# Y's and the turn's products alternated on four quarters of the array, in the chunked recurrence of a two-layer decoder

## The chip, the cores and the metric

The kernel runs on one core of a Trainium2 chip. The metric is the device time of one execution in microseconds. A core has TensorE (PE; its weight loads are shown apart as PEld), VectorE (DVE), ScalarE (ACT), GpSimd (POOL) and SyncE (SP), which issues the DMAs here. TensorE multiplies a stationary operand (`lhsT`) with a moving one (`rhs`) and writes into PSUM; its array can be used in parts: rows follow the partitions of the operands, columns those of the output.

## The reference

A decoder trunk of two layers on 2048 tokens of 1024 channels in fp32: sliding-window attention, then RWKV-7 time mixing, each with a gated branch and a per-layer embedding. The change is in the second layer's recurrence, one 64x64 state for each of 16 heads:

```python
def step(S, inp):
    r_t, d_t, k_t, v_t, kk_t, a_t = inp
    sa = jnp.einsum('bhvk,bhk->bhv', S, -kk_t)
    S = S * d_t[:, :, None, :] + sa[..., None] * (kk_t * a_t)[:, :, None, :] + v_t[..., None] * k_t[:, :, None, :]
    y = jnp.einsum('bhvk,bhk->bhv', S, r_t)
    return S, y
...
mean = jnp.mean(y, axis=-1, keepdims=True)
var = jnp.mean(jnp.square(y - mean), axis=-1, keepdims=True)
y = ((y - mean) * lax.rsqrt(var + GN_EPS)).reshape(B, T, C) * gn_g.astype(jnp.float32) + gn_b.astype(jnp.float32)
bonus = jnp.sum(r4 * k4 * r_k.astype(jnp.float32), axis=-1, keepdims=True) * v4
y = (y + bonus.reshape(B, T, C)).astype(h.dtype)
return (y * jax.nn.silu(z)) @ w_out
```

## The kernel before

Four phases follow each other; the last, `rwkv` (line 1165), holds all that the diff touches but one line. It works in chunks of 64 tokens (`LC`), 32 of them (`NCH`). Channels lie on partitions, 128 to a tile, so a tile column p (8 of them, `NP`) holds two heads, one on each half of the partitions (`half`); h and eo number the halves.

Within a chunk the recurrence is solved in closed form, in small fp32 products. Each fp32 product is two matmul instructions on the chip, called passes below. `chain(c)` (line 1323) runs them: r1p from the state and the chunk's values (line 1329); the first part of y (1335); `turn` (1365), which transposes the normed y of the chunk before, `yc`, to channels on partitions; up, through the inverted triangle `tt` (1341); two copies of u into `uv`, one on VectorE and one on ScalarE (1342, 1343); sp, the state's update (1348), which VectorE and GpSimd carry on; and y's second part (1356). y's and the turn's and up's products are 64x64, with the rows and the columns of the same half; r1p, sp and y's second part use all rows and one half of the columns.

Three generators feed the chain. `front(c)` (1221) makes the chunk's products `aps` (16 passes for each of two halves of p) and transposes its keys; the chain needs it a chunk later. `tri(g)` (1253) inverts the triangles of four chunks: 30 steps of two VectorE operations (1269, 1271), then for each chunk a first and a second set of 32x32 products `wq` (1290, 1300) with copies `wt` and `tt` behind them, one half on ScalarE and one on VectorE. `output(c, y)` (1372) norms y, waits for its turn, multiplies by `gn_g` and adds and multiplies by `bvt` and `szt`, which `load_bz` (1360) loads, and stores `gated`.

Between these products stands the dense work of the layer, one step of three 128x128x512 matmuls at a time (`mm3`, lines 589 to 591), from `Dense.run` (143): the z projection, the output projection, the gate. `self.ticks(n)` lets every running generator make n steps, so `STEPS` (1321) says how many dense steps stand behind r1p, behind y and turn, behind up and behind the end of the chain: 18 for a chunk. `add_gate1` (403) has at line 418 a number of such steps between the gate's elementwise work and four transposes on TensorE.

The program is built with a plan by simulated time (line 1451): within an engine's queue instructions may be put ahead of others that the plan has waiting. Each queue then runs in that order. PSUM tiles of tag "f" come from 3 buffers, "ch" (r1p, up, sp) from 1, y from 1.

## Time and profile before

| what | value |
|---|---|
| median of 3 runs | 3070.1 us (3067.87 to 3070.78) |
| the profiled execution | 3072.72 us, span 3070.6 us |
| granted TensorE clock over the span | 0.969 |
| TensorE busy | 2865.7 us, 93% |
| VectorE busy | 1950.4 us, 64% |
| ScalarE, GpSimd busy | 43%, 33% |
| 16 DMA engines, hardware queue | 69.8% |

The share of an engine is over the whole span, with its four phases; what a change in one phase is worth is read from that phase. A row of the timeline gives the start in us from the span's start, the length in us, the engine, the line, the operation, what it writes and reads, shapes, and how many instructions were merged; its length runs to the end of the last one, and since matmuls are pipelined the next one starts before that. In brackets stands how long the engine was idle before and what it waited for. PEclk is the granted TensorE clock, 1.00 being 2.4 GHz.

### The profile page before, as it was taken

Reading aid. Unit: us, or ns where it says so; the run is one execution under the profiler, and the core shown is the slowest. Engines: PE = TensorE matmul, PEld = TensorE weight load, DVE = VectorE, ACT = ScalarE, POOL = GpSimd, SP = SyncE. Lnnn points to the kernel's source line nnn. Section 1 sums busy time; section 2 is a strip of 40 time slices with the busy share of each in tenths; the row PEclk is TensorE's granted clock in tenths of the full one; section 3 lists DMA queues with packets and bytes.
Section 4 is the critical chain, followed back from the end, with each engine's and each line's share of the span. In section 5 each row is a group of like instructions: output and inputs, shape, how many; then the busy total and the mean of one; then the engine's idle time right before and its main releaser. Section 6 shows DMA issues by size and latency. Waiting matters only on the chain. (4 is left out here: it accounts for less than half of the span.)

```text
span 3070.6 us, 56425 instructions
## 1 busy us (share of the span) xinstructions
PE 2865.7 (93%) x21416; PEld 2265.5 (74%) x21416; DVE 1950.4 (64%) x3529; ACT 1314.0 (43%) x2840; POOL 1005.2 (33%) x886
## 2 busy tenths in 40 slices
PE   7999998999999999898998799888989989999987
PEld 5888886777777777686776588666777767777766
DVE  6532434775777655738678965588685795784444
ACT  5311114784465543526677733322334433332422
POOL 2242510001211232404556600224445435435421
PEclk9999999999999999999999899999999999999999
DMA  7664857999886687636556778896779878679574
GB/s 224 187 144 107 167 142 224 308 284 335 253 258 207 214 270 244 192 114 199 176 190 197 213 209 207 244 285 177 190 198 253 217 228 242 170 209 249 164 250 158
DMA packets 622687, 652.41 MB, mean 212 GB/s; under 512 B 259152, under 2 KB 433360, under 8 KB 622416
## 3 DMA queue, kind: packets, MB, share of 16 engines
q1 hardware_dynamic: 614736, 638.31, 69.8%
q0 software_dynamic: 7680, 10.50, 3.1%
q8 instruction: 169, 2.77, 0.4%
q14 instruction: 102, 0.84, 0.1%
HBM read 421.39 MB, written 216.79 MB: 208 GB/s over the span
## 5 line engine op out<-in xcount | busy, mean ns | idle before, releaser
L589 PE MATMUL ps<-dhi,dwh 128*128 128x512 f32 x1472 | 610.1, 416 | 23.4 <-ACT dwh L538 9.9
L591 PE MATMUL ps<-dhi,dwl 128*128 128x512 f32 x1472 | 590.6, 402 | 11.5 <-DVE dwl L540 11.0
L590 PE MATMUL ps<-dlo,dwh 128*128 128x512 f32 x1472 | 592.6, 404 | 4.3 <-DVE dlo L540 2.4
L589 PE MATMUL ps<-xH,wh 128*128 128x512 f32 x1408 | 554.2, 400 | 17.7 <-DVE kb L1071 11.2
L590 PE MATMUL ps<-xL,wh 128*128 128x512 f32 x1408 | 560.2, 398 | 5.0 <-POOL xL L540 4.0
L591 PE MATMUL ps<-xH,wl 128*128 128x512 f32 x1408 | 561.2, 399 | 1.3 <-DVE wl L540 1.3
L589 PEld LDWEIGHTS ps<-dhi,dwh 128*128 128x128 f32 x1472 | 281.1, 191 | 95.5 <-ACT dwh L538 11.4
L591 PEld LDWEIGHTS ps<-dhi,dwl 128*128 128x128 f32 x1472 | 281.5, 191 | 78.5 <-DVE dwl L540 13.8
L590 PEld LDWEIGHTS ps<-dlo,dwh 128*128 128x128 f32 x1472 | 281.8, 192 | 61.8 <-DVE dlo L540 4.5
L589 PEld LDWEIGHTS ps<-xH,wh 128*128 128x128 f32 x1408 | 267.9, 191 | 80.4 <-DVE kb L1071 14.9
L590 PEld LDWEIGHTS ps<-xL,wh 128*128 128x128 f32 x1408 | 269.2, 191 | 67.4 <-POOL xL L540 7.3
L591 PEld LDWEIGHTS ps<-xH,wl 128*128 128x128 f32 x1408 | 269.0, 191 | 59.2 <-DVE wl L540 2.6
L699 POOL DMA_DIRECT2D t<-t x160 | 126.1, 1274 | 200.2 <-issue 75.6
L873 ACT ACTIVATE S<-S,nm 128x256 f32<-128x256 f32 (+1 forms) x256 | 125.5, 492 | 66.1 <-DVE nm L870 59.3
L540 POOL TENSOR_TENSOR xL<-xs,xH 128x512 fp32r<-128x512 f32 x72 | 109.8, 1535 | 76.0 <-ACT xH L538 73.0
L538 ACT ACTIVATE wh<-wr 128x1024 fp32r<-128x1024 f32 x44 | 46.6, 1059 | 190.9 <-DMA wr<-in_attn_w_in 144.9
L864 DVE CUSTOM_DVE_ANT_0 S<-sc,mask,sink 128x256 f32<-128x256 f32 (+1 forms) x256 | 108.7, 469 | 23.4 <-PE sc L860 23.2
L1269 DVE TENSOR_TENSOR tmp<-P 128x30 f32<-128x30 f32 (+14 forms) x240 | 111.7, 466 | 13.8 <-POOL P L1260 7.5
L1052 POOL TENSOR_TENSOR kb<-kb,mhalf 128x16 f32<-128x16 f32 x32 | 100.6, 3146 | 36.9 <-DVE kb L1051 36.6
L1271 DVE TENSOR_TENSOR P<-P,tmp 128x30 f32<-128x30 f32 (+14 forms) x240 | 108.2, 451 | 6.7
L975 DVE SCALAR_TENSOR_TENSOR xs<-hp,mu,xs 128x512 f32<-128x512 f32 x96 | 93.1, 986 | 28.8 <-ACT xs L974 28.5
L540 POOL TENSOR_TENSOR dlo<-z,dhi 128x512 fp32r<-128x512 f32 x16 | 22.3, 1408 | 258.8 <-ACT dhi L538 252.2
(258 smaller groups left out, 5211.6 us busy)
## 6 DMA issues: line engine op xcount, KB each, us to landing
hp<-hn SPq DMA_DIRECT2D x72, 256.5 KB, 4.3
sz<-th SPq DMA_DIRECT2D x64, 256.0 KB, 4.4
ple<-pt SPq DMA_DIRECT2D x64, 256.0 KB, 7.1
aux<-ple SPq DMA_DIRECT2D x64, 256.0 KB, 5.3
yd<-kx SPq DMA_DIRECT2D x32, 512.0 KB, 4.2
dwh<-wp_ao SPq DMA_DIRECT2D x24, 512.0 KB, 6.1
dwl<-wp_ao SPq DMA_DIRECT2D x24, 512.0 KB, 6.8
dwh<-wp_ag SPq DMA_DIRECT2D x24, 512.0 KB, 4.5
```

The source lines that it names most:

```text
L538: nc.scalar.activation(hi, src, AF.Copy)
L540: e.tensor_tensor(out=lo, in0=src, in1=f32(hi), op=ALU.subtract)
L589: mm(ps, lhsT=wh, rhs=ah, start=first, stop=False)
L590: mm(ps, lhsT=wh, rhs=al, start=False, stop=False)
L591: mm(ps, lhsT=wl, rhs=ah, start=False, stop=last)
L699: nc.gpsimd.dma_start(out=t1[32 * d:32 * d + 32, :], in_=t2[32 * a:32 * a + 32, :], accum_op=ALU.add)
L864: nc.vector.tensor_tensor_reduce(out=S[:, i, c0:], in0=sc[:, eo, c0:], in1=mask[:, c0:], scale=1.0, scalar=sink[:, 4 * g + 2 * j + eo:4 * ...
L873: nc.scalar.activation(S[:, i, c0:], S[:, i, c0:], AF.Exp, bias=nm[:, i:i + 1], accum_out=den[:, i:i + 1])
L975: nc.vector.scalar_tensor_tensor(out=src, in0=t[:, :G], scalar=mus[:, c, k:k + 1], in1=src, op0=ALU.mult, op1=ALU.add)
L1052: nc.gpsimd.tensor_tensor(out=bs[:, :, 0], in0=bs[:, :, 0], in1=self.mhalf.broadcast_to([128, m]), op=ALU.pow)
L1269: nc.vector.tensor_tensor(out=t, in0=P[:, 0:r, r:r + 1].broadcast_to([128, r, n]), in1=P[:, r:r + 1, r + 1:].broadcast_to([128, r, n]), op ...
L1271: nc.vector.tensor_tensor(out=P[:, 0:r, r + 1:], in0=P[:, 0:r, r + 1:], in1=t, op=ALU.add)
```

## The change

The y products and the turn's products are issued in turns, two of y (on the quarters of the diagonal) and two of the turn, and the turn writes its result to the other half of the partitions, so that it uses the two other quarters. What follows it lies with its halves swapped: `gn_g` has a swapped copy `gnx`, and `bvt`, `szt` and the store of `gated` are two DMAs each (`heads`); the last chunk keeps the old way. Up follows directly, without ticks between. The first half of `aps` of chunk c+2 is issued at the end of chain(c), behind y's second part, and the second half behind r1p of chain(c+1); y's second part and `aps` take half 1 first. The `wq` products of two chunks of a group are issued together, and their copies are all on ScalarE. `load_front` stands ahead of the chain, and the gate's transposes come two steps later.

```diff
@@ -415,7 +415,7 @@
             if ct == 0:
                 sums[n] = self.cp.tile([128, NB, KT], F32, name="ss", bufs=2)
             ss = sums[n]
-            for _ in range(4):
+            for _ in range(6):
                 yield
             for b in range(NB):
                 nc.tensor.transpose(ps[:, b * 128:b * 128 + 128], th[:, b * 128:b * 128 + 128], tr.ident)
@@ -1196,13 +1196,16 @@
             p_f, p_c, p_y = (self.pool(es, "pw_" + nm, b, PSUM) for nm, b in (("f", 3), ("c", 1), ("y", 1)))
             dense.transposed = lambda name: p_f.tile([128, G], F32, name=name, tag="f")
             gng = self.vec["gn_g"]
+            gnx = cp.tile([128, NP], F32, name="gnx")
             dl = self.decay
             if "decay" in self.override:
                 nc.sync.dma_start(out=dl, in_=self.override["decay"])
             S = cp.tile([128, NP, 64], F32, name="S0")
             nc.vector.memset(S, 0.0)
             half = (slice(0, 64), slice(64, 128))
-            AM, X1, XA, BN, TT, UV, AG, BZ, YC, YT = {}, {}, {}, {}, {}, {}, {}, {}, {}, {}
+            for h in range(2):
+                nc.sync.dma_start(out=gnx[half[1 - h]], in_=chan(ins["rwkv_gn_g"][0], NP)[half[h]])
+            AM, X1, XA, BN, TT, UV, AG, BZ, YC, YT, FR = {}, {}, {}, {}, {}, {}, {}, {}, {}, {}, {}
 
             def load_front(c):
                 x1 = X1[c] = x1p.tile([128, NP, 128], F32, name="x1")
@@ -1226,7 +1229,7 @@
                 for i in range(NP // 4):
                     pse = [p_f.tile([128, 4, 128], F32, name="aps", tag="f") for eo in range(2)]
                     for j in range(4):
-                        for eo in range(2):
+                        for eo in (1, 0):
                             nc.tensor.matmul(pse[eo][:, j], lhsT=x1[half[eo], 4 * i + j], rhs=xa[half[eo], 4 * i + j],
                                              start=True, stop=True)
                     for eo in range(2):
@@ -1281,28 +1284,27 @@
                 for e in range(2):
                     nc.gpsimd.memset(tt[64 * e + 32:64 * e + 64, :, :, 0:32], 0.0)
                 yield
-                for j in range(TG):
-                    wt = sm.tile([128, NP, 32], F32, name="wt")
+                for j in range(0, TG, 2):
+
+
+                    wt = sm.tile([128, 2, NP, 32], F32, name="wt")
                     wq = p_f.tile([128, 2, NP, 32], F32, name="wq", tag="f")
-                    for p in range(NP):
-                        for e in range(2):
-                            r0 = 64 * e
-                            nc.tensor.matmul(wq[r0 + 32:r0 + 64, 0, p], lhsT=ag[r0:r0 + 32, p, j, 32:64], rhs=at[r0:r0 + 32, p, j],
-                                             start=True, stop=True)
+                    ops = [(i, p, 64 * e) for i in range(2) for p in range(NP) for e in range(2)]
+                    for i, p, r0 in ops:
+                        nc.tensor.matmul(wq[r0 + 32:r0 + 64, i, p], lhsT=ag[r0:r0 + 32, p, j + i, 32:64], rhs=at[r0:r0 + 32, p, j + i],
+                                         start=True, stop=True)
                     for e in range(2):
-                        cpy = nc.vector.tensor_copy if e else nc.scalar.copy
-                        cpy(wt[64 * e + 32:64 * e + 64], wq[64 * e + 32:64 * e + 64, 0])
-                    yield
-                    yield
-                    for p in range(NP):
-                        for e in range(2):
-                            r0 = 64 * e
-                            nc.tensor.matmul(wq[r0:r0 + 32, 1, p], lhsT=wt[r0 + 32:r0 + 64, p], rhs=tt[r0 + 32:r0 + 64, p, j, 32:64],
-                                             start=True, stop=True)
+                        nc.scalar.copy(wt[64 * e + 32:64 * e + 64], wq[64 * e + 32:64 * e + 64])
+                    for _ in range(4):
+                        yield
+                    for i, p, r0 in ops:
+                        nc.tensor.matmul(wq[r0:r0 + 32, i, p], lhsT=wt[r0 + 32:r0 + 64, i, p], rhs=tt[r0 + 32:r0 + 64, p, j + i, 32:64],
+                                         start=True, stop=True)
                     for e in range(2):
-                        cpy = nc.vector.tensor_copy if e else nc.scalar.copy
-                        cpy(tt[64 * e:64 * e + 32, :, j, 32:64], wq[64 * e:64 * e + 32, 1])
-                    TT[g * TG + j] = tt[:, :, j]
+                        nc.scalar.copy(tt[64 * e:64 * e + 32, :, j:j + 2, 32:64],
+                                       wq[64 * e:64 * e + 32].rearrange("q i p t -> q p i t"))
+                    for i in range(2):
+                        TT[g * TG + j + i] = tt[:, :, j + i]
                     yield
                 if (g + 1) * TG < NCH:
                     load_ab(g + 1)
@@ -1318,7 +1320,7 @@
                     nc.sync.dma_start(out=uv[half[1 - eo], eo], in_=vn[eo, c * LC:c * LC + LC, :].rearrange("t (p d) -> t p d", d=64))
                 UV[c] = uv
 
-            STEPS = (2, 2, 4, 10)
+            STEPS = (4, 4, 10)
 
             def chain(c):
                 uv, am, tt, bn, xa = UV.pop(c), AM.pop(c), TT.pop(c), BN.pop(c), XA.pop(c)[:, :, :, c % 2]
@@ -1329,19 +1331,27 @@
                     mm(r1p[half[eo], p], lhsT=am[:, p, eo, 0:LC], rhs=uv[:, eo, p], start=True, stop=True)
                 r1 = r2.tile([128, NP, 64], F32, name="r1")
                 nc.scalar.copy(r1, r1p)
+                if c + 1 < NCH:
+                    next(FR[c + 1])
+                    self.live.append(FR.pop(c + 1))
                 self.ticks(STEPS[0])
                 y = p_y.tile([128, NP, 64], F32, name="y")
-                for p, eo in pairs:
-                    mm(y[half[eo], p], lhsT=xa[half[eo], p, 1], rhs=uv[half[eo], eo, p], start=p == 0, stop=False)
                 if c:
-                    turn(c - 1, YC.pop(c - 1))
-                self.ticks(STEPS[1])
+                    yc, tp = YC.pop(c - 1), p_f.tile([128, NP, LC], F32, name="ytp", tag="f")
+                for p in range(NP):
+                    for h in range(2):
+                        mm(y[half[h], p], lhsT=xa[half[h], p, 1], rhs=uv[half[h], h, p], start=p == 0, stop=False)
+                    for h in range(2 if c else 0):
+
+                        mm(tp[half[1 - h], p], lhsT=yc[half[h], p], rhs=self.ident[half[h], half[h]], start=True, stop=True)
+                if c:
+                    YT[c - 1] = tp
                 up = p_c.tile([128, NP, 64], F32, name="up", tag="ch")
                 for p, eo in pairs:
                     mm(up[half[eo], p], lhsT=tt[half[eo], p], rhs=r1[half[eo], p], start=True, stop=True)
                 nc.vector.tensor_copy(uv[half[0], 0], up[half[0]])
                 nc.scalar.copy(uv[half[1], 1], up[half[1]])
-                self.ticks(STEPS[2])
+                self.ticks(STEPS[1])
                 if c + 1 < NCH:
                     sp = p_c.tile([128, NP, 64], F32, name="sp", tag="ch")
                     for p, eo in pairs:
@@ -1353,24 +1363,36 @@
                         nc.vector.tensor_tensor(out=UV[c + 1][half[eo], eo], in0=t[half[eo]], in1=d[half[eo]], op=ALU.mult)
                     nc.gpsimd.tensor_tensor(out=S, in0=t, in1=d, op=ALU.mult)
                 for p, eo in pairs:
-                    mm(y[half[eo], p], lhsT=am[:, p, eo, LC:], rhs=uv[:, eo, p], start=False, stop=p == NP - 1)
+                    mm(y[half[1 - eo], p], lhsT=am[:, p, 1 - eo, LC:], rhs=uv[:, 1 - eo, p], start=False, stop=p == NP - 1)
+                if c + 2 < NCH:
+                    FR[c + 2] = front(c + 2)
+                    next(FR[c + 2])
                 self.start(output(c, y))
-                self.ticks(STEPS[3])
+                self.ticks(STEPS[2])
 
             def load_bz(c):
                 BZ[c] = tuple(r2.tile([128, NP, LC], F32, name=nm) for nm in ("bvt", "szt"))
                 for t, src in zip(BZ[c], (bv, sz)):
-                    nc.sync.dma_start(out=t, in_=src[:, c * LC:c * LC + LC].rearrange("(p q) t -> q p t", q=128))
-
-            def turn(c, yc):
-
-                tp = YT[c] = p_f.tile([128, NP, LC], F32, name="ytp", tag="f")
+                    for h, a in heads(c, src):
+                        nc.sync.dma_start(out=t[h], in_=a)
+
+            def heads(c, ap):
+
+
+                a = ap[:, c * LC:c * LC + LC].rearrange("(p q) t -> q p t", q=128)
+                if c + 1 == NCH:
+                    return [(slice(0, 128), a)]
+                return [(half[1 - h], a[half[h]]) for h in range(2)]
+
+            def turn(yc):
+
+                tp = p_f.tile([128, NP, LC], F32, name="ytp", tag="f")
                 for p in range(NP):
                     for h in half:
                         nc.tensor.matmul(tp[h, p], lhsT=yc[h, p], rhs=self.ident[h, h], start=True, stop=True)
+                return tp
 
             def output(c, y):
-                t0 = c * LC
                 bvt, szt = BZ.pop(c)
                 sq = r2.tile([128, NP, 64], F32, name="sq")
                 nc.scalar.activation(sq, y, AF.Square)
@@ -1384,19 +1406,20 @@
                     YC[c] = yc
                     while c not in YT:
                         yield
+                    tp, gn = YT.pop(c), gnx
                 else:
                     for _ in range(4):
                         yield
-                    turn(c, yc)
-                tp = YT.pop(c)
-                nc.vector.tensor_tensor(out=yc, in0=tp, in1=gng.rearrange("q (p o) -> q p o", o=1).broadcast_to([128, NP, LC]), op=ALU.mult)
+                    tp, gn = turn(yc), gng
+                nc.vector.tensor_tensor(out=yc, in0=tp, in1=gn.rearrange("q (p o) -> q p o", o=1).broadcast_to([128, NP, LC]), op=ALU.mult)
                 e = nc.gpsimd if c + 1 < NCH else nc.vector
                 e.tensor_tensor(out=yc, in0=yc, in1=bvt, op=ALU.add)
                 e.tensor_tensor(out=yc, in0=yc, in1=szt, op=ALU.mult)
                 if c + 1 == NCH:
                     dense.rest = yc
                     return
-                nc.sync.dma_start(out=gated[:, t0:t0 + LC].rearrange("(p q) t -> q p t", q=128), in_=yc)
+                for h, a in heads(c, gated):
+                    nc.sync.dma_start(out=a, in_=yc[h])
                 self.outputs = c + 1
 
             load_front(0)
@@ -1404,21 +1427,22 @@
             self.start(tri(0))
             self.start(front(0))
             load_front(1)
+            FR[1] = front(1)
+            next(FR[1])
             uv_tile(0)
             for eo in range(2):
                 nc.gpsimd.memset(UV[0][half[eo], eo], 0.0)
             for c in range(NCH):
                 if c + 1 < NCH:
                     uv_tile(c + 1)
-                    self.start(front(c + 1))
                 if c % TG == 1 and c + TG - 1 < NCH:
                     self.start(tri(c // TG + 1))
                 while c not in TT or c not in AM or z_cols(c // GC) < KT:
                     self.tick()
                 load_bz(c)
-                chain(c)
                 if c + 2 < NCH:
                     load_front(c + 2)
+                chain(c)
             self.drain()
 
     def run(self, phases=None):
```

## Rows read from the trace of the kernel before

**Rows 1.** Busy time by chunk: stretch, length, PE, PEld, DVE, ACT, POOL, PEclk, DMA.
```profile
2275.66:2304.28 28.62, 25.22 (x286) 20.41 (x286) 27.44 (x47) 6.59 (x12) 11.27 (x10) 0.94 0.59 158
2304.28:2327.60 23.32, 23.32 (x288) 18.73 (x287) 8.52 (x14) 7.49 (x13) 11.19 (x10) 1.00 0.98 239
2327.60:2356.28 28.68, 28.68 (x543) 22.66 (x541) 12.76 (x19) 16.75 (x30) 17.54 (x15) 1.00 0.94 252
2356.28:2385.82 29.54, 25.71 (x290) 20.57 (x289) 24.55 (x43) 9.51 (x16) 10.54 (x11) 0.94 1.02 278
```

**Rows 2.** TensorE's waits, 2050 to 2932 us: us in total, times, longest.
```profile
PE y L1356 <- DVE uv L1342: 19.7, 8, 5.2
PE ps L421 <- DVE th L327: 8.1, 5, 2.6
```

**Rows 3.** Timeline of TensorE, an fp32 product of 512 columns in the first phase.
```profile
54.57 1.02 PE L658 MATMUL rb<-dg,ones 128*128 128x512 f32 x2
55.43 0.82 PE L672 MATMUL tp<-ident,xt 128*128 128x128 f32 x6
```

**Rows 4.** Timeline of TensorE, 2302 to 2311 us.
```profile
2302.63 0.39 PE L590 MATMUL ps<-dlo,dwh 128*128 128x512 f32 x1
2302.86 0.40 PE L591 MATMUL ps<-dhi,dwl 128*128 128x512 f32 x1
2303.19 1.16 PE L1230 MATMUL aps<-xa,x 64*128 64x128 f32 x16
2304.28 1.15 PE L1329 MATMUL r1p<-uv,am 128*64 128x64 f32 x32
2305.36 0.50 PE L589 MATMUL ps<-dhi,dwh 128*128 128x512 f32 x1
2305.70 0.40 PE L590 MATMUL ps<-dlo,dwh 128*128 128x512 f32 x1
...
2308.69 1.15 PE L1335 MATMUL y<-uv,xa 64*64 64x64 f32 x32
2309.67 1.10 PE L1370 MATMUL ytp<-ident,yc 64*64 64x64 f32 x32
2310.70 0.50 PE L589 MATMUL ps<-dhi,dwh 128*128 128x512 f32 x1
```

**Rows 5.** Timeline of TensorE, 2331 to 2344 us, wq products.
```profile
2331.57 0.69 PE L1290 MATMUL wq<-at,ag 32*32 32x32 f32 x32
...
2342.59 0.54 PE L1290 MATMUL wq<-at,ag 32*32 32x32 f32 x22
2342.94 0.22 PE L1300 MATMUL wq<-tt,wt 32*32 32x32 f32 x2
2342.96 0.22 PE L1290 MATMUL wq<-at,ag 32*32 32x32 f32 x3
...
2343.57 1.15 PE L1348 MATMUL sp<-uv,bn 128*64 128x64 f32 x32
```

**Rows 6.** Timeline, 2314 to 2320 us, ScalarE's and TensorE's rows.
```profile
2314.65 0.58 ACT L1343 COPY uv<-up 64x512 f32<-64x512 f32 x1 [1.91 <-DVE uv L1342]
...
2319.17 0.33 PE L1356 MATMUL y<-uv,am 128*64 128x64 f32 x2
2319.43 0.49 PE L590 MATMUL ps<-dlo,dwh 128*128 128x512 f32 x1
2319.85 1.15 PE L1348 MATMUL sp<-uv,bn 128*64 128x64 f32 x32
```

**Rows 7.** Groups by line, VectorE, 2050 to 2932 us: busy us, mean ns, idle before.
```profile
L1304 DVE COPY tt<-wq 32x256 f32<-32x256 f32 x30 | 12.7, 422 | 27.8 <-ACT tt L1304 27.3
```

**Rows 8.** Timeline of SP's queue, 2316 us.
```profile
2316.97 0.65 SPq L1363 DMA_DIRECT2D bvt<-bv  x1
```

**Rows 9.** Timeline of TensorE, 2290 to 2299 us.
```profile
2294.35 0.30 PE L1356 MATMUL y<-uv,am 128*64 128x64 f32 x2 [3.00 <-DVE P L1271]
...
2295.00 1.98 PE L1348 MATMUL sp<-uv,bn 128*64 128x64 f32 x32
```

## The prediction

> **What bounds the kernel now.** I read the busy shares first, then the recurrence alone (line 1165 on), cut into its 64-token chunks at each first r1p product, then the order on TensorE inside a chunk, then the waits. The recurrence fills about 2050 to 2930 us of the span. In the table by chunk [rows 1] there are two kinds. The stretch at 2304.28 lasts 23.32 us and TensorE is busy for all 23.32; the one at 2327.60, which has the small wq products in it, 28.68 of 28.68. The stretch at 2275.66 lasts 28.62 us with TensorE at 25.22 and VectorE at 27.44: there the triangular solve's products on VectorE (lines 1269 and 1271) set the pace. Of the 30 stretches of that table 19 have TensorE at 94% or more of their length and 11 have not. So TensorE time taken out counts in some two thirds of the chunks, and in the rest VectorE keeps most of it. The longest single cause of TensorE's waits is the copy of u on VectorE, 19.7 us in 8 waits [rows 2].
>
> **How TensorE spends a chunk.** The stretch has 18 ticks of dense work (54 products at 0.23 us) and islands of small fp32 products. An fp32 product is two passes: one full-array pass of 512 columns took 0.43 us (0.86 us for the two, until the next instruction) [rows 3], so 0.84 ns a column, and 64 columns are 54 ns. The y products on two quarters of the array are 32 passes in 0.98 us until the turn starts [rows 4]; one after the other they would be 32 x 54 ns = 1.72 us, so two quarters run side by side. The turn then takes 1.03 us until the next dense product. An island also has edges: the step from the dense product to aps is 0.33 us instead of 0.23 (+0.10), r1p takes 1.08 us until the dense product instead of y's 0.98 (+0.10), and the first dense product takes 0.34 instead of 0.23 (+0.11) [rows 4]. So 0.31 us for each island between dense products.
>
> **The change, part by part.**
> *Y and turn on four quarters* (lines 1334 to 1337). Now the two are run one after the other, each on the two quarters of the diagonal: 0.98 + 1.03 = 2.01 us [rows 4]. After it the turn uses the other two quarters and the products alternate. If four run side by side, 64 passes last as long as one of the two now, 1.03 us: 0.98 us less per chunk. If they don't, 0. What speaks for four: where the two kinds of wq products meet, products of line 1300 start at 2342.94 us between those of line 1290 at 2342.59 and 2342.96, on other 32x32 tiles, and the 64 passes take 0.98 us until sp, while 32 of one kind alone span 0.69 [rows 5]. I take 0.98. The Trainium skill, "TensorE: Matmul & The Clock Gate", section "Part 3: Packing small matmuls", speaks against it: weight loads are to overlap running matmuls only where the row group differs, and y and turn share row groups. By it the gain here would be 0. The trace doesn't bear it out: r1p's two column halves use all rows and still make 32 passes in 1.08 us, not 1.72 [rows 4]. The same page's floor of 25 ns between starts ("Wait — 56ns, not 53.3ns?") would give 64 x 25 = 1.6 us, a gain of 0.41; the 64 wq passes in 0.98 us are 15 ns each [rows 5], against it.
>
> *Fewer islands.* Now a chunk has: aps with r1p; the other aps; y with turn; up; one lone y product (2 passes, then a dense product) ahead of sp; sp with y [rows 4, 6]. That is 6 (the x transposes don't change). After it: r1p with aps; y, turn and up; sp, y and the next chunk's aps: 3. The lone y product runs first because it needs only VectorE's copy of u; with half 1 first it needs ScalarE's, which is released by VectorE's [rows 6], so I expect it gone in half of the chunks or more: 2.5 islands fewer. One more change of shape lies inside an island (y to aps), which no row shows by itself; I take half an edge, 0.15 us, between 0 and 0.31. So 2.5 x 0.31 - 0.15 = 0.63 us a chunk; ends 2 x 0.31 - 0.31 = 0.31 and 3 x 0.31 = 0.93.
>
> *wq products of two chunks in one run.* 4 of 8 runs fewer for each group of four chunks, 7 groups: 28 edges between 0.15 (run joined to another island) and 0.31; I take 0.2: 5.6 us, in chunks where TensorE is full.
>
> *wt and tt copies all on ScalarE.* VectorE loses some 30 copies of each kind (12.7 us for the tt ones [rows 7]). ScalarE is busy for 6.6 to 16.8 us of a chunk [rows 1], which covers it. It falls in the wq chunk, where VectorE has 12.76 of 28.68 us: 0. If ScalarE were late, the wait would stand before the second wq products, which have four ticks (2.8 us) for copies of 0.4 us.
>
> *Two more ticks before the gate's transposes* (line 418). TensorE waited 8.1 us there for th, in 5 waits [rows 2]. Two dense ticks are 1.4 us each, some 6 us in all; but most lie in chunks where VectorE is late anyway. I take 2, ends 0 and 8. The PSUM tile is held 1.4 us longer, out of three.
>
> *Swapped halves.* bvt, szt and the gated store become two DMAs each: 3 more issues a chunk on SP's queue, 0.65 us each by one of bvt's now [rows 8], some 2 us a chunk. Behind them on that queue stand the loads of x and of dense weights. None of TensorE's longer waits is for a DMA [rows 2], so the loads have time in hand. Bytes stay. I take 0; the loss has no end on its own but is the second rival. The load of x moves ahead of the chain; it already lands a chunk early, so 0.
>
> *The rest* (the order of the two halves in aps, two small loads of gn_g once): 0, nothing waits for either.
>
> *Order of waits.* Aps of chunk c+2 moves to the end of chunk c, behind y; it needs x loaded by then and two PSUM buffers. Up now stands straight behind the turn, so a turn that waits for its PSUM buffer delays up and through it the copies of u; that wait is short now and I take 0.
>
> *Sum.* In 19 chunks 0.98 + 0.63 = 1.61 us: 30.6. In the 11 others VectorE holds the chunk; of its idle 1 to 5 us a part is waiting for TensorE, and I take a quarter of the saving, 0.4 x 11 = 4.4. With 5.6 and 2: 42.6 us. The profiled execution took 3072.7 us (span 3070.6 and 2.1 around it): 3072.7 - 42.6 = 3030.1. It lay 2.6 us above the median of the runs, so 3027.5; I give 3027.
>
> **Rivals.**
> *No fourfold overlap*, either by the array or because the order that the compiler's planner makes takes y and turn apart again. The 0.98 falls away: 19 x 0.63 = 12.0, 2 in the others, 5.6 and 2: 21.6, so 3049. With the low island price, 19 x 0.31 + 4 = 10: 3060. For it: no row shows four 64x64 quarters. Against it: [rows 5].
> *DMA takes TensorE's place.* In the stretches with a full TensorE the DMA share is 0.94 to 0.98, and 1.02 at 278 GB/s in the one at 2356.28 [rows 1]. Shorter chunks need the same bytes in 7% less time, and the three more issues delay weights. 12 of the 19 full stretches have a share of 0.84 or more; if these keep their length, 12 x 1.61 = 19.3 us are lost: 3047. Against it: 278 GB/s is above the 239 x 23.3 / 21.7 = 257 needed.
> *Slower: the clock.* At 2294.35 us, after 3.00 us of idle, sp took 1.98 us instead of 1.15 [rows 6, 9] and the granted clock of that stretch is 0.94 [rows 1]: part of it went at the lower of its two levels, 1.2 GHz for 2.4. The new island of sp, y and aps is the longest one, some 3 us of small products with no dense one between. If the clock fell in it, it would lose 3 x 0.83 = 2.5 us; in all 31 chunks 77 us, 35 more than the gain: 3070.1 + 35 = 3105. It decides from 42.6 / 2.5 = 17 chunks on. Against it: the stretch at 2304.28 has its clock at 1.00 [rows 1] with all these products in it, and the fall shown follows idle time, which the change doesn't add where TensorE is full.
> *Nothing measurable*: the planner's order moves waits as much as edges are saved, 3065 to 3075.
>
> **How the numbers follow.** Forecast 0.60; no overlap 0.13; DMA 0.12; nothing 0.07; slower by the clock or a new wait 0.08. Low end: saved in all 31 chunks, 31 x 1.61 + 5.6 + 8 = 63.5, so 3007, and half of what islands at 0.93 would add (31 x 0.30 = 9.3) less: 3002. High end: no overlap at the low price, 3060. Under 0.2% (6 us) no change can be told. Faster by more: 0.60, nearly all of 0.25, a little of the rest, 0.84; same 0.07; slower 0.09.
>
> **What would show it.** Y and turn together in 1.0 to 1.1 us on the timeline, not 2.0: the first step. Up directly behind them, no dense product between y and sp, aps behind y: the second. Chunks with a full TensorE at 21.5 to 22 us, those of VectorE at 28 to 30 as before: the sum. Weight loads as TensorE's releaser: the second rival. More stretches with PEclk under 1.00: the third. It would be wrong above all if the chunks of VectorE shrank too, or if the first step gave nothing.

## The result, and the profile after

The changed kernel takes 3082.0 us (median of 5 runs, 3079.5 to 3084.6) where the kernel before took 3067.9 beside it (3060.6 to 3070.8): a ratio of 1.0053, interval 1.0041 to 1.0064, so 14 us slower. The forecast was 3027, 43 us faster, and its range ended at 3060.

The profiled execution of the kernel after spans 3079.2 us. Its chunks, from one first r1p product to the next (columns as in [rows 1]):

```profile
2239.09:2278.31 39.22, 27.92 (x287) 21.13 (x286) 38.33 (x61) 12.04 (x21) 18.97 (x16) 0.78 0.61 162
2278.31:2305.42 27.11, 23.81 (x288) 19.59 (x287) 20.75 (x31) 7.90 (x14) 12.66 (x11) 0.94 0.53 137
2305.42:2327.63 22.21, 22.21 (x287) 18.06 (x286) 7.14 (x11) 7.31 (x13) 9.29 (x8) 1.00 1.04 269
2327.63:2358.07 30.44, 28.31 (x541) 22.61 (x540) 8.68 (x11) 17.10 (x29) 17.07 (x14) 0.94 0.96 251
```

A chunk with a full TensorE takes 22.21 us where it took 23.32 [rows 1]: 1.1 us less. Such chunks, with TensorE at 94% or more, are 14 of the 30 now; 19 were counted before. The chunk at 2239.09, which lies in a solve, takes 39.22 us; VectorE is busy for 38.33 of them and TensorE for 27.92, at a mean clock of 0.78.

TensorE's waits from 2050 to 2935 us (us in total, times, longest):

```profile
PE sp L1358 <- ACT uv L1353: 43.6, 10, 9.1
PE ps L421 <- DVE th L327: 18.1, 6, 5.3
PE ps L589 <- ACT dhi L538: 13.4, 3, 5.4
```

The wait put down to the copy of u has grown from 19.7 to 43.6 us, and the gate's wait for th from 8.1 to 18.1 [rows 2]. Before, some of the waits at this place are put down to other instructions; all waits of sp and of y's second part together went from 30.6 to 46.6 us, all waits on lines 421 and 589 to 591 from 15.7 to 35.1. So the products became shorter and the waits longer. To set one against the other I added up TensorE's time between the second and the last start of sp, from instruction to instruction, with the part in which the trace's record of the granted clock has the lower level, 1.2 GHz. "At full clock" takes half of that part off (a dense product takes 0.43 us there, 0.23 at the higher level, so this is slightly too much). The two columns on the right are experiments from below.

| us | before | after | b_ag | a_ag |
|---|---|---|---|---|
| stretch | 827.8 | 839.4 | 808.2 | 773.5 |
| TensorE occupied | 766.8 | 743.7 | 759.7 | 721.3 |
| of it at 1.2 GHz | 59.5 | 100.3 | 48.2 | 52.2 |
| occupied, at full clock | 737.1 | 693.6 | 735.6 | 695.2 |
| idle | 61.0 | 95.7 | 48.5 | 52.2 |

At full clock TensorE's own work fell by 43.5 us. That lies near the forecast's 42.6 by luck: the forecast counted eleven chunks at a quarter, and by its own terms the work of these 29 chunks falls by 29 x 1.61 + 5.6 = 52 us. Against the 43.5 stand 34.7 us more of idle time and 20.4 us more of low clock (half of 40.8): 11.6 us longer in this stretch.

Where that happens is seen when the time is cut at the solves instead of at the chunks: from the transpose that begins a solve (line 1262, 1259 before) to the end of the transposes into tt, and from there to the next solve. Columns again as in [rows 1]. Before, two solves and two stretches between:

```profile
2186.20:2242.33 56.13, 55.24 (x807) 44.03 (x806) 23.33 (x39) 19.29 (x36) 27.69 (x24) 0.97 0.82 224
2242.33:2300.98 58.65, 50.58 (x600) 40.13 (x600) 56.09 (x89) 18.21 (x33) 27.36 (x25) 0.94 0.67 188
2300.98:2359.51 58.53, 58.53 (x897) 46.19 (x897) 24.90 (x40) 26.73 (x48) 33.60 (x28) 1.00 0.94 247
2359.51:2410.40 50.89, 43.61 (x509) 35.37 (x506) 47.84 (x81) 14.85 (x23) 17.56 (x16) 0.93 0.81 214
```

The same four after:

```profile
2173.05:2231.66 58.61, 56.80 (x855) 46.47 (x854) 20.53 (x31) 20.80 (x37) 24.50 (x21) 0.94 0.96 239
2231.66:2292.44 60.78, 47.99 (x567) 37.04 (x565) 58.52 (x91) 18.49 (x33) 30.14 (x27) 0.86 0.57 159
2292.44:2358.07 65.63, 61.69 (x922) 50.01 (x922) 22.75 (x31) 27.75 (x48) 33.91 (x28) 0.95 0.90 232
2358.07:2407.71 49.64, 37.46 (x479) 30.06 (x478) 47.29 (x81) 14.92 (x24) 17.35 (x16) 0.92 0.80 215
```

In the second and fourth line of each VectorE is busy for 94 to 96% of the time, whatever TensorE does. Over the six solves from 2100 us on they take 322.5 us before and 317.1 after, while TensorE's idle time inside them goes from 40.5 to 66.6 us and the dense products of lines 589 to 591 that run there fall from 588 to 535. The five stretches between them, where TensorE should have gained, went from 304.9 to 322.1 us: 632 dense products instead of 588 (44 x 0.23 = 10 us), 11 us more idle, 23 us more at the low clock (11.5 us lost by it). The shorter small products make up for only a part of that.

The solve reads its input from a tile (ag) that is loaded through SP's queue when the solve before has been used up. SP's queue of the kernel after, ahead of one such load (us from the start, length, line):

```profile
2341.43 1.36 SPq L1215 DMA_DIRECT2D x<-yd  x2
2342.89 2.17 SPq L1377 DMA_DIRECT2D bvt<-bv  x2
2345.16 2.69 SPq L1377 DMA_DIRECT2D szt<-sz  x2
2347.90 1.31 SPq L1422 DMA_DIRECT2D gated<-yc  x2
2349.30 1.53 SPq L84 DMA_DIRECT2D raw<-gated  x2
2350.93 0.38 SPq L1314 DMA_DIRECT2D ag<-ab  x1
```

And the chain of waits of that kernel, from that issue on (start, length, what):

```profile
2350.93 7.12 DMA ag<-ab
2358.05 0.02 issue
2358.07 2.22 DVE P L1262
2360.35 2.13 POOL P L1263
```

The last wq product that reads the old ag starts at 2342.3 us; the load is issued at 2350.93, behind the six transfers of bvt, szt and gated, which are split in pairs, and four others. Before, the last of those products starts at 2349.2 and the load is issued at 2350.98: TensorE came 7 us earlier, and the next solve 1.4 us. These products in the kernel after and in the kernel before (shortest, median and longest in ns; first and last start), and the load before:

```profile
L1294 PE MATMUL wq<-at,ag x128: 191/191/212, 2333.6 to 2342.3; 32*32 32x32 f32 x128
L1290 PE MATMUL wq<-at,ag x128: 190/191/213, 2331.6 to 2349.2; 32*32 32x32 f32 x128
2350.98 0.38 SPq L1312 DMA_DIRECT2D ag<-ab  x1
```

VectorE's wait for this load, after and before, 2050 to 2935 us:

```profile
DVE P L1262 <- DMA ag<-ab: 19.0, 5, 7.7
DVE P L1259 <- DMA ag<-ab: 13.2, 6, 4.1
```

This became the last theory; the ones that I tried first are told in their order.

### The profile page after: what moved, and what is told of

Same layout as the page of the kernel before. It is cut to its first block, busy times and chain, and to the rows that moved or that the text cites. A ratio compares the mean times of both kernels' runs of the same rounds, so it can differ in the third digit from the quotient of the medians.

```text
span 3079.2 us, 56446 instructions
## 1 busy us (share of the span) xinstructions
PE 2840.4 (92%) x21416; PEld 2254.4 (73%) x21416; DVE 1923.1 (62%) x3465; ACT 1327.5 (43%) x2840; POOL 1004.6 (33%) x886
## 5 line engine op out<-in xcount | busy, mean ns | idle before, releaser
L589 PE MATMUL ps<-dhi,dwh 128*128 128x512 f32 x1472 | 609.7, 416 | 29.9 <-ACT dhi L538 17.5
L589 PE MATMUL ps<-xH,wh 128*128 128x512 f32 x1408 | 555.0, 400 | 17.2 <-DVE kb L1071 8.7
L591 PEld LDWEIGHTS ps<-xH,wl 128*128 128x128 f32 x1408 | 269.2, 191 | 59.5 <-DVE wl L540 2.6
L538 ACT ACTIVATE wh<-wr 128x1024 fp32r<-128x1024 f32 x44 | 46.6, 1058 | 185.4 <-DMA wr<-in_attn_w_in 142.5
L1272 DVE TENSOR_TENSOR tmp<-P 128x30 f32<-128x30 f32 (+14 forms) x240 | 105.4, 439 | 13.2 <-POOL P L1263 7.0
```

The source lines that it names most:

```text
L589: mm(ps, lhsT=wh, rhs=ah, start=first, stop=False)
L591: mm(ps, lhsT=wl, rhs=ah, start=False, stop=last)
L1272: nc.vector.tensor_tensor(out=t, in0=P[:, 0:r, r:r + 1].broadcast_to([128, r, n]), in1=P[:, r:r + 1, r + 1:].broadcast_to([128, r, n]), op ...
```

## Experiments

Each run stood beside the kernel before on the same chip; the ratio is to that.

**One part at a time undone.** The theory at first was that up, now with 12 dense products instead of 23 between it and sp, leaves too little cover for the copy of u.

*a_steps486*, dense ticks from behind y2 to behind up:

```diff
-            STEPS = (4, 4, 10)
+            STEPS = (4, 8, 6)
```

> The changed kernel with four steps more between up and sp and four fewer behind the chain (4, 8, 6 for 4, 4, 10), 18 as before. Cover theory: in the kernel before, the queue of TensorE had some 23 dense products between up and sp, in the changed one 12 and part of aps, which run in 4.0 us for 6.0; so sp stands waiting for the copies of u wherever VectorE is late. With 24 dense products there again, sp's wait for the copies falls from 43.6 us to under 25, chunks with a full TensorE stay near 22.2 us, the clock falls less often, and the time is 3030 to 3055 us. Rival (VectorE is late whatever TensorE does, because of the solve): the wait moves on to r1p, behind which now only 6 steps stand, and the time stays at 3075 to 3090.

*a_aps_head*, the first half of aps back at the head of its chunk (from behind y2 to ahead of the chain):

```diff
-                if c + 2 < NCH:
-                    FR[c + 2] = front(c + 2)
-                    next(FR[c + 2])
...
+                    if c:
+                        FR[c + 1] = front(c + 1)
+                        next(FR[c + 1])
```

> The changed kernel with the first half of aps back at the head of the next chunk, ahead of r1p, instead of behind y at the end of the chain; all else as changed. Cover theory: what took the dense products away from between up and sp is aps, which the planned order puts there in their place; with aps at the head the built order has 25 or so dense products there again, sp's wait falls to under 25 us and the time is 3030 to 3055. Rival: the wait comes from the copies and the wq products of two chunks, or from VectorE alone; then 3075 to 3090.

*a_gate4*, four ticks again ahead of the gate's transposes (line 418):

```diff
-            for _ in range(6):
+            for _ in range(4):
```

> The changed kernel with the gate's transposes 4 steps behind as before, not 6. Cover theory: within 6 us of the changed kernel (3076 to 3088), since TensorE's wait for th (18.1 us, 8.1 before) grew because VectorE's work was pushed back, not because of the two steps. Rival: the two steps brought the transposes next to other waits; then the wait for th falls to 8 and the time to 3070 or less.

*a_wq_single*, wq and its copies as before (lines 1287 to 1307, here their head):

```diff
-                for j in range(0, TG, 2):
+                for j in range(TG):
```

> The changed kernel with the wq products of one chunk at a time and their copies on both engines, as before. Cover theory: sp's wait for the copies of u stays above 35 us and the time within 3078 to 3095, some 5 us more for the extra islands. Rival: wq of two chunks and the copies on ScalarE alone delay the chain in the chunks that hold them; then sp's wait falls to 30 or less and the time to 3065 or less.

Measured: 1.0076 (1.0056 to 1.0096), 1.0072 (1.0044 to 1.0101), 1.0064 (1.0046 to 1.0082), 1.0042 (1.0028 to 1.0057). None gives the loss back. TensorE's waits in a_steps486:

```profile
PE sp L1358 <- ACT uv L1353: 29.9, 11, 5.0
PE ps L589 <- ACT dhi L538: 22.1, 7, 7.2
PE ps L421 <- DVE th L327: 13.2, 7, 2.5
PE r1p L1331 <- DVE uv L1363: 10.7, 10, 3.7
```

The wait that the edit aims at shrank from 43.6 to 29.9 us and others took its place; TensorE idles 98.7 us from 2050 to 2930 us as it did in the kernel after (98.3). The cover theory falls: a wait that only moves was not the cause.

**Without the solve, and each half of the change on the kernel before.** a_nosolve and b_nosolve leave out the products and sums of the solve in either kernel (the part of the result that it gives is not computed):

```diff
-                    nc.vector.tensor_tensor(out=t, in0=P[:, 0:r, r:r + 1].broadcast_to([128, r, n]),
...
-                    nc.vector.tensor_tensor(out=P[:, 0:r, r + 1:], in0=P[:, 0:r, r + 1:], in1=t, op=ALU.add)
```

> The kernel after, without the 60 VectorE instructions of each triangular solve (the products and additions of its steps are left out, so the part of the result that the solve gives is not computed; every product of TensorE, copy, DMA and turn of the generators stays). To be set against the kernel before with the same left out. Theory VectorE: in the chunks of a solve VectorE and what queues on it hold the time, so that what TensorE saves becomes waiting there and the clock falls after it; without the solve every chunk gains as the full chunks do (1.1 us x 31 = 34 us, and some 5 us of the paired wq runs), so this kernel is 25 to 45 us faster than the one before without its solve, and TensorE's idle time from 2050 us on falls from 98 us to under 50. Rival order: the new order (first half of the next chunk's aps moved, up directly behind) makes the waits by itself; then this kernel is still as slow as the one before without its solve (within 8 us) or slower, and idles some 30 us longer than that.

> The kernel before, without the 60 VectorE instructions of each triangular solve (same part left out). Theory VectorE: it falls below the kernel before by what VectorE holds there, some 30 to 60 us, and is 25 to 45 us slower than the changed kernel without its solve. Rival order: within 8 us of the changed kernel without its solve, or faster than it.

*b_alt* puts the alternation alone on the kernel before, with the transfers and the second gain that it needs (after's lines 1199 to 1207, 1340 to 1348, 1376 to 1393, 1409 to 1422), *b_front* the order of front alone (1334 to 1336, 1367 to 1369, 1430 to 1445). Their cores:

```diff
-                for p, eo in pairs:
-                    mm(y[half[eo], p], lhsT=xa[half[eo], p, 1], rhs=uv[half[eo], eo, p], start=p == 0, stop=False)
                 if c:
-                    turn(c - 1, YC.pop(c - 1))
+                    yc, tp = YC.pop(c - 1), p_f.tile([128, NP, LC], F32, name="ytp", tag="f")
+                for p in range(NP):
+                    for h in range(2):
+                        mm(y[half[h], p], lhsT=xa[half[h], p, 1], rhs=uv[half[h], h, p], start=p == 0, stop=False)
+                    for h in range(2 if c else 0):
+                        mm(tp[half[1 - h], p], lhsT=yc[half[h], p], rhs=self.ident[half[h], half[h]], start=True, stop=True)
```

```diff
+                    next(FR[c + 1])
+                    self.live.append(FR.pop(c + 1))
...
+                    FR[c + 2] = front(c + 2)
+                    next(FR[c + 2])
...
-                    self.start(front(c + 1))
```

> The kernel before with the alternation alone: y's and the turn's products in one run of 32 + 32 on four quarters, and with it the swapped halves, the split transfers of bvt, szt and gated, and the second copy of the gain; ticks 2, 2, 4, 10, front, wq and gate as before. Theory VectorE: 0.98 us less of TensorE in each of 31 chunks, of which the chunks with a solve give back most: 0 to 20 us faster than before (ratio 0.993 to 1.000). Rival order: its cover between up and sp is before's (23 dense products), so all of it is kept: 25 to 31 us faster (ratio 0.990 to 0.992). Rival transfers: the split transfers and the later output cost what the change lost: slower than before by 5 us or more.

> The kernel before with the order of front alone: the first half of the aps products two chunks ahead behind the second y, the second half directly behind r1p, the loads of the next chunks ahead of the chain; y, turn, up's ticks, wq and gate as before. Some 20 islands fewer (0.3 us each: 6 us of TensorE). Theory VectorE: within 8 us of before. Rival order: this is what makes the waits: slower than before by 10 to 40 us (ratio 1.003 to 1.013), TensorE idle from 2050 us on up from 62 us to over 85.

Measured: a_nosolve 2998.3 and b_nosolve 3003.5 us, 0.9775 (0.9750 to 0.9800) and 0.9789 (0.9759 to 0.9819): without the solve's arithmetic the change is worth 5 us, not 25 to 45; the two intervals overlap, so even the 5 can't be told from nothing. The change is no longer a loss there. TensorE's first waits in a_nosolve are for the operands of the dense products:

```profile
PE ps L421 <- DVE th L327: 13.4, 3, 7.1
PE ps L589 <- ACT dhi L538: 10.2, 4, 7.3
```

So VectorE's arithmetic in the solve, taken away, is not enough to let the gain through; the theory that it alone takes it falls by its own number. What I read in these two traces only later: the transpose that began the solve is still there, and it waits for its load 33.7 us in a_nosolve and 16.9 in b_nosolve:

```profile
DVE P L1262 <- DMA ag<-ab: 33.7, 6, 8.8
DVE P L1259 <- DMA ag<-ab: 16.9, 6, 5.5
```

Its fourth to eighth start at 2211.3, 2319.1, 2414.3, 2542.5 and 2630.0 us in the one and at 2208.4, 2316.8, 2413.7, 2542.4 and 2633.7 in the other, shorter chunks or not; what stands behind it in VectorE's queue waits with it. b_alt gives 0.9996 (0.9983 to 1.0010), b_front 1.0083 (1.0053 to 1.0113): the alternation alone gained nothing that can be told, and front's order alone cost 25 us. In b_front the aps runs take 77.8 us instead of 71.1 (from second to last sp, as in the table above). Some pieces of two or four aps products are cut off from the rest; the four here take 0.42 us until the dense product, where sixteen took 1.09 [rows 4]:

```profile
2202.69 0.49 PE L1230 MATMUL aps<-xa,x 64*128 64x128 f32 x4
2203.11 0.51 PE L589 MATMUL ps<-dhi,dwh 128*128 128x512 f32 x1
```

**Front's order undone in the kernel after, and a slower solve.** *a_nofront* takes b_front's lines (its diff above, turned round) back out of the kernel after; the three kernels with *spread* let the solve give way after each step, so it hands VectorE two instructions a tick instead of four:

```diff
-                    if r % 2:
-                        yield
+                    yield
```

> The kernel after with before's order of front (both halves of the next chunk's aps from the head of the chunk on, loads behind the chain); the alternation, up directly behind it, the paired wq and six gate ticks stay. 25 to 27 dense products stand between up and sp in most chunks instead of 12. Theory front: front's order, which alone made the kernel before 25 us slower, is what loses; without it the kernel keeps the alternation (about 1 us a chunk in the full chunks) and is 10 to 25 us faster than before (ratio 0.992 to 0.997). Rival feed: VectorE and what queues on it hold some 12 chunks whatever TensorE saves; then what is saved becomes waiting again and it is within 8 us of before (ratio 0.997 to 1.003).

> The kernel after with the solve spread out: its generator gives way after each step instead of after every second one, so 2 VectorE instructions a tick instead of 4, over some 30 ticks instead of 15. Theory VectorE burst: the chunks in which the solve runs wait because the chain's VectorE instructions queue behind it; sp's wait (43.6 us) falls to under 20 and the kernel gains 15 to 40 us, to below the kernel before. Rival feed: the waits go over to the operands of the dense products and the time moves by less than 8 us.

> The kernel before with the same spreading alone. Theory VectorE burst: its wait of the second y for uv (19.7 us) shrinks and it gains 5 to 25 us. Rival feed: within 8 us of before.

> The kernel after with before's order of front and the spread solve. If front's order and the burst both cost, it is the fastest of all: 25 to 50 us faster than before (ratio 0.984 to 0.992). If the feed holds the chunks, it stands within 8 us of before.

Measured: a_nofront 1.0053 (1.0037 to 1.0070), as slow as the kernel after, so front's order is not what loses there. a_spread 0.9996 (0.9981 to 1.0012): the same instructions less densely, and all of the loss is regained. b_spread 1.0020 (1.0005 to 1.0036): the same edit costs the kernel before 7 us. a_nofront_spread 0.9965 (0.9950 to 0.9979). So how the solve lies among VectorE's work matters to the kernel after, and not its arithmetic alone. In a_spread VectorE waits longer for the solve's input than in the kernel after (19.0 us), though it is the faster kernel, so the length of this wait alone doesn't measure the loss:

```profile
DVE P L1262 <- DMA ag<-ab: 35.3, 6, 9.0
```

Still, it led to the load.

**The solve's input loaded early.** *a_ag* and *b_ag* split ag in two tiles of half the size. The half that the solve transposes is loaded again directly behind that transpose, some 100 us ahead; the half that wq reads is loaded as before. ScalarE writes ab in another order in the phase before, so that each half is one transfer.

```diff
-                ag = AG.pop(g)
+                ag0, ag = AG.pop((g, 0)), AG.pop((g, 1))
...
-                nc.vector.transpose(PT, ag.rearrange("q p c t -> q t (p c)")[:, 0:32])
+                nc.vector.transpose(PT, ag0.rearrange("q p c t -> q t (p c)"))
+                if (g + 1) * TG < NCH:
+                    load_ah(g + 1, 0)
...
-                    load_ab(g + 1)
+                    load_ah(g + 1, 1)
```

> The kernel after, with the solve's input loaded earlier: ag is kept as two tiles of half the size, and the half that the solve transposes is loaded again as soon as that transpose has read it, some 100 us before its next use (in exchange ScalarE writes ab in another order in the phase before). It takes away the wait of the solve's first instruction for its load (19 us in 5 waits). Theory span: from the third solve on, VectorE is 95% busy in the six solves (317 us, as 322 before), and what lies between them has grown from 305 to 322 us, in part because the next solve begins late; then the stretches between shrink and the kernel is 8 to 20 us faster than after (ratio to before 0.999 to 1.003). Rival: the late load is beside the point, and the time stays within 5 us of after.

> The kernel before with the same earlier load (its wait there is 13 us). Theory span: 3 to 15 us faster than before. Rival: within 3 us.

*a_nofront_spread_ag* puts it on a_nofront_spread; *a_nofront_wide* on a_nofront, with the solve's generator started a chunk earlier and giving way three times for two steps:

```diff
+                    yield
                     if r % 2:
                         yield
...
-                if c % TG == 1 and c + TG - 1 < NCH:
+                if c % TG == (c < TG) and c // TG + 1 < NCH // TG:
```

> The kernel after with before's order of front, the solve spread over 30 ticks and ag loaded earlier (its wait there is 37 us in 6 waits). Theory span: the solves begin up to 6 us earlier each: 5 to 25 us faster than the one without the earlier load (3058.5), 15 to 35 us below before. Rival: within 5 us of 3058.5.

> The same, but from the third solve on the solve starts one chunk earlier and gives way three times for two steps (45 ticks, so four chunks carry it instead of three). Theory span: with VectorE's work spread more evenly, more dense products run beside the solve, TensorE idles less than 60 us from 2050 us on, and the kernel is 25 to 50 us faster than before (ratio 0.984 to 0.992), the fastest. Rival: VectorE's other work (operands of the dense products) holds the time, and it stays within 5 us of 3058.5.

| | us | ratio to before |
|---|---|---|
| b_ag | 3056.9 | 0.9949 (0.9931 to 0.9967) |
| a_ag | 3024.7 | 0.9843 (0.9821 to 0.9865) |
| a_nofront_spread_ag | 3030.1 | 0.9870 (0.9849 to 0.9890) |
| a_nofront_wide | 3020.7 | 0.9838 (0.9815 to 0.9860) |

With the early load the change is worth 32 us (3056.9 to 3024.7), and a_ag is faster than both kernels. It gained 57 us on the kernel after by the medians (64 by the ratios), far more than the 8 to 20 expected and more than the 19 us of the wait itself. The trace shows what changed besides: with its input there, the built order puts each solve directly behind the one before, ahead of the wq products of that one. The fourth starts at 2142 us instead of 2232, and from it on each takes 104 to 118 us instead of 44 to 61. a_ag, three solves on end (columns as in [rows 1]):

```profile
2142.31:2252.45 110.14, 100.30 (x1351) 79.39 (x1350) 80.55 (x123) 41.39 (x73) 64.06 (x54) 0.96 0.83 218
2252.45:2356.92 104.47, 97.45 (x1444) 77.80 (x1442) 68.75 (x112) 42.67 (x74) 51.94 (x45) 0.98 0.87 231
2356.92:2462.90 105.98, 97.66 (x1402) 79.20 (x1403) 78.35 (x124) 44.90 (x79) 49.17 (x40) 0.95 0.89 231
```

VectorE is 66 to 74% busy in them, not 95. The wait that began this is down from 43.6 to 23.9 us, and the wait for ag is gone (VectorE now waits 17.6 us for the wq products that free `at`, a tile the solve writes at its end):

```profile
PE sp L1364 <- ACT uv L1359: 23.9, 8, 7.3
PE ps L589 <- ACT dhi L538: 7.8, 6, 3.3
PE ps L421 <- DVE th L327: 7.4, 4, 2.9
```

TensorE's idle time is 52.2 us and its low clock 52.2, near b_ag's 48.5 and 48.2, and its work at full clock is 40 us below b_ag's (table above). The profiled execution of b_ag took 3068.0 us, 11 more than its median, but its first r1p product starts 10 us later than in the kernel before (1993.8 for 1983.9), so that much of it lies ahead of the stretch of the table. A part of the gain is paid ahead of it too: a_ag is 65.9 us shorter than the kernel after in the stretch, and 55.3 in the whole span (3023.9 for 3079.2), since its second sp starts 10 us later. How much is the load's wait and how much the solve's new place was not separated. Spreading it further is not told apart: a_nofront_wide stands within a_ag's interval.

**Which part carries the 32 us.** The alternation alone, and front's order alone, on b_ag:

> The kernel before with the earlier load and the alternation alone (swapped halves, split transfers; ticks, front, wq and gate as before). With the late load the alternation alone gave -2 us. Theory late load: the gain of the first step was there and was lost in the solves; with the earlier load it stays, 0.6 to 1.0 us in each of 31 chunks: 15 to 31 us faster than the kernel before with the earlier load (which stands at ratio 0.995), ratio 0.985 to 0.990. Rival: the 32 us between the two kernels with the earlier load come from the other parts; then it is within 6 us of 0.995.

> The kernel before with the earlier load and front's order alone. With the late load front's order alone cost 25 us. Theory late load: most of that came from solves that begin late; with the earlier load it is within 8 us of the kernel before with the earlier load (ratio 0.992 to 0.998). Rival: the cost is of the order itself (aps runs of TensorE grew by 7 us, the wait for uv from 20 to 46 us); then it is 15 to 30 us slower than that (ratio 1.000 to 1.005).

b_alt_ag 0.9913 (0.9899 to 0.9928) and b_front_ag 0.9980 (0.9968 to 0.9993), against b_ag's 0.9949: 11 us gained and 10 us lost. The first lies between its two theories, the second at the end of the late load's range. Part of what front's order cost with the late load (25 us) was the load's, part is its own: aps takes 77.8 us there against b_ag's 71.0. And 11 us are less than the 30 of the first step: in the order built for b_alt_ag, y, turn and the transposes of x fall by 18.7 us only (130.9 to 112.2), in a_ag by 31.9 (to 99.0). The rest of the 32 us comes from up behind the turn, paired wq and gate, or from the parts in company (between dense products stand 207 runs of small ones in b_ag's stretch, runs of x's transposes alone left out, 211 in b_alt_ag, 170 in b_front_ag, 138 in a_ag). Which of these stays open.

## Why the prediction was wrong, point by point

**Y and turn on four quarters: right.** Timeline of TensorE after, the end of such a run:

```profile
2842.31 0.22 PE L1346 MATMUL ytp<-ident,yc 64*64 64x64 f32 x1
2842.32 0.22 PE L1343 MATMUL y<-uv,xa 64*64 64x64 f32 x1
2842.36 0.22 PE L1346 MATMUL ytp<-ident,yc 64*64 64x64 f32 x1
2842.37 0.22 PE L1343 MATMUL y<-uv,xa 64*64 64x64 f32 x1
...
2842.55 1.03 PE L1351 MATMUL up<-r,tt 64*64 64x64 f32 x28
```

From 2841.62 to 2842.43 us 52 passes went by in 0.81 us, 15.6 ns each, and up follows directly. y, turn and x's transposes together took 100.7 us instead of 132.4 in 29 chunks: 1.09 us a chunk, 0.98 forecast. So the first rival falls. The rule weighed with it (the Trainium skill, "TensorE: Matmul & The Clock Gate", section "Part 3: Packing small matmuls": weight loads overlap running matmuls only where the row group differs) doesn't hold for these products: y and turn share row groups, and the passes start 15.6 ns apart.

**Fewer islands: sized too high.** The full chunk lost 1.1 us, not 1.61, about what y and turn gave by themselves, so little is left of the islands' 0.63. The lone y product is gone and no dense product stands between y and sp, but a piece of aps is often left alone behind y: at 2849.62 two aps products take 0.42 us until the next dense one, and the aps runs grew from 71.1 to 80.1 us (5 of the 9 are low clock: 14.2 us at it instead of 4.2).

**wq in pairs, gate: nothing to be told.** a_wq_single and a_gate4 stand within the interval of the kernel after. The gate's wait rose from 8.1 to 18.1 us where I took 2 off.

**Swapped halves at 0: for a wrong reason.** It was that no wait of TensorE is for a DMA [rows 2]. That a load could be late for VectorE I didn't ask: VectorE's own waits were not read, and the load of ag stood in them (13.2 us before, 19.0 after), behind those issues on the queue (fence above). TensorE then waits for VectorE's and ScalarE's copies, and no row of its waits names the DMA. That the splitting made the load late is not shown: of the 8.6 us from the last wq product to the load's issue the second transfers of the three pairs take 2.0 (0.73, 0.64 and 0.63), and in b_alt, which has them too, VectorE waits 15.8 us for ag, 2.6 more than before.

**"A quarter of the saving" in the eleven other chunks: the step that failed.** It took these chunks as a part of the time that TensorE's saving could still enter, and the 19 others as untouched by them. Most of them lie in spans of one VectorE job, some 44 to 62 us each, that mostly begins when a load lands. What TensorE saves in a span that it doesn't set is idle time there (66.6 instead of 40.5 us); after the idle time the clock fell (sums at 1.2 GHz 59.5 to 100.3 us; in the chunk at 2239.09 TensorE is idle for 11.3 us and the clock is 0.78); and what didn't run there (535 dense products for 588) runs later, in chunks that were to keep their whole saving; the full ones are 14 of the 30 now, not 19. The solves together became 5.4 us shorter, the stretches between them 17.2 longer, so the sign was minus, not a quarter of plus. With the solve's input early, in a new order of the solves, the same change gives 32 us of the 42.6. Whether the late load or the dense solve does more of the harm stays open: a_spread takes back the loss though its wait for the load is longer.

**Rivals.** Slower by the clock came nearest, though not as told: the clock didn't fall in the new island of sp, y and aps (1.00 in the chunk at 2305.42, which has it) but behind idle time, and a rival that says "the change adds idle time where VectorE holds" would have been the one to write. No DMA took TensorE's place directly: none is among its longer waits.

## What to carry to other kernels

Before a saving on a busy engine is counted, cut the time where the slowest job of the *other* engines begins and ends, not only at the loop's turns, and ask what starts that job: a load behind a queue, a buffer. Read the waits of the second busiest engine as well as those of the first. A change that is right and gives nothing can be the second half of one: here a load of 7 us, moved ahead, with the order that came of it, turned 14 us lost into 47 gained against the kernel before, to which the load alone gives 15.

## What the runs showed of the hardware that I had not expected

Four 64x64 quarters with two different moving operands run at 15.6 ns a pass, in the same row groups. A step of the solve took very different times for like sizes: before, VectorE's product of 128x84 at 2250.66 us took 0.99 us and its sum of the same size at 2252.24 0.23 us, while GpSimd ran to 2251.55 and again from 2253.05 (VectorE's rows, then GpSimd's):

```profile
2250.66 0.99 DVE L1269 TENSOR_TENSOR tmp<-P 128x84 f32<-128x84 f32 x1
2251.57 0.74 DVE L299 SCALAR_TENSOR_TENSOR xs<-xs,mu,raw 128x512 f32<-128x512 f32 x1
2252.24 0.23 DVE L1271 TENSOR_TENSOR P<-P,tmp 128x84 f32<-128x84 f32 x1
...
2253.18 1.28 DVE L1269 TENSOR_TENSOR tmp<-P 128x130 f32<-128x130 f32 x1
2248.50 3.05 POOL L298 TENSOR_TENSOR xs<-raw 128x512 f32<-128x512 f32 x3
2253.05 1.27 POOL L540 TENSOR_TENSOR dlo<-xs,dhi 128x512 fp32r<-128x512 f32 x1 [1.50 <-ACT dhi L538]
```

That the one holds up the other is what the times suggest; it was not tried. The Trainium skill, "SBUF — State Buffer", section "Who interferes with whom", states it for a VectorE instruction with two inputs in SBUF beside a GpSimd one that reads there; these rows agree with it. And a profile of the kernel after whose TensorE is busy for 25 us less than before (2840.4 for 2865.7 us) can belong to the slower kernel.
